# Attention and squared-ReLU MLP on one core: pinned weight splits, down-projection halves taken in turn two blocks apart, paced output sums

## The chip, the cores and the metric

The kernel runs as one program on 1 core of one Trainium2 chip. The metric is the time of one execution on the device, in microseconds (us). Of the kernel before there are three timed runs, from 2081.25 to 2085.26 us, with a median of 2083.21 us, and one profiled execution.

The engines are named as in the profile: PE (matmul), PEld (its weight loads), DVE (VectorE), ACT (ScalarE), POOL (GpSimd) and SP (SyncE, which here issues the loads).

## The reference

One layer: attention over an 8 x 64 grid of tokens, then an MLP with a squared ReLU. The change is in the MLP alone.

```python
D_MODEL, SEQ, MLP_HIDDEN = 2048, 512, 8192

def sq_relu_mlp(h, w1, w2):
    a = jax.nn.relu(h @ w1)
    return (a * a) @ w2

x = x + neighbourhood_attention(rms_norm(x, norm_mix), ...)
x = x + sq_relu_mlp(rms_norm(x, norm_mlp), mlp_w1, mlp_w2)
```

## The kernel before

**Number format.** All matmuls work on float32 values that are split in two parts, h (a rounded copy) and l (the rest), and each product is three matmuls: h·h, h·l and l·h. So every weight tile has to be split on the chip before PE can use it: ACT writes `wh` (line 233), DVE writes `wl` (line 235).

**The MLP in pairs.** Both projections are cut in a form of Strassen's scheme with seven products instead of eight (M1 to M7). A *pair* (class `Pair`) makes two column tiles of the result, 2 x 512 columns, for all 512 tokens. Its inner dimension is cut into *blocks* of four row tiles; for each block and each of the seven products there is one *chunk*, which is 12 matmuls (line 248). A pair goes through two stages: first M1, M5, M6, M4 for each of its blocks, and then M2, M3, M7 for each. With four blocks that is 28 chunks. The products share PSUM banks x, z, y and w (table `BANK`); at the last block of a product its bank is evicted (`evict`). M5, M6, M4 and M7 take a sum of weight quarters that is kept up as a chain (table `CHAIN`): DVE adds the quarter just loaded and the sum of the product before it in place, in line 217, before the split. So 4 of the 7 chunks of a block need this *add* (16 of the 28 in a pair).

**Up projection.** Pairs h0 to h7 multiply by `w1`, each with four blocks. Their results go through the ReLU, are turned on PE by eight small tasks per pair (`left_window`, run by `window()` in the second stage of the next pair), squared, and written by POOL to `z_t` in DRAM as sixteen blocks, two per pair, together with the sums that Strassen's left side needs.

**Down projection.** The sixteen blocks of z are used four at a time: `zc[c]` for c = 0 to 3. For each c there are two pairs, one for each half of the output's columns, named in the trace as tiles of `y`: y0_0, y0_1, y1_0, ... y3_1. After each chunk of y0_1, y1_1 and y2_1 (and of h7, for c = 0), `pass_on` loads the z tile that will take the place of the one just used for the last time: SP loads `zr` (line 759, 128 x 512), and six steps later `split_left` splits it as ACT's `a_z...h` (line 554) and DVE's `a_z...l` (line 556). So h7, y0_1, y1_1 and y2_1 carry 28 such loads and splits each, the other pairs none. Here such a pair is called a pair *with hand-over*.

**Output.** Every pair of c = 0 to 2 adds its eight output tiles to `y_sum` in DRAM with an accumulating DMA from POOL (line 748), as soon as each is evicted. The pairs of c = 3 read `y_sum` back (`prefetch`), add it and write `out`.

**What sets the order.** The program is written as chunks with side tasks that are due some *steps* later; a chunk is four steps. `run` issues the weight loads six chunks ahead and starts a split three chunks ahead. In `split_raw` the add is written first, `wh` five steps later and `wl` two steps after that. But the order in which instructions stand on each engine is not the written one: a scheduler sorts them, except those marked by `kept`, which keep the program's order. Before, `kept` has an effect only in the first 32 steps of the program.

**Buffers.** Weights land in the pool `raw` (10 tiles of 128 x 1024), split weights are in `hl` (3 pairs), and almost all else, the z tiles and the output tiles included, is in `tiles` (70 tiles of 128 x 512).

```python
def split_raw(u, i, first):
    ...
        if m in u.CHAIN:
            nc.vector.tensor_tensor(out=s, in0=s, in1=u.raw[u.CHAIN[m], b], op=ALU.add)
        yield 5 * STEP
    h = hl.tile([P, 2, T], F32R, tag="wh", name=f"wh_{name}")
    l = hl.tile([P, 2, T], F32R, tag="wl", name=f"wl_{name}")
    ...
        kept(nc.scalar.activation(h, s, AF.Copy))
        yield 2 * STEP
        kept(nc.vector.tensor_tensor(out=l, in0=s, in1=h.bitcast(F32), op=ALU.subtract))
```

Of the kernel before, what the change touches and what calls it, by code (L numbers as in the profile page):

```python
# [25 lines left out]
NCH = HID // D  # L26
# [6 lines left out]
NB = KT // 4  # L33
# [8 lines left out]
STEP, WAIT, PAIR = 1, 5, 3  # L42


class Unit:
# [7 lines left out]
    def __init__(self, name, src, act, done, kind):  # L53
        self.name, self.src, self.act, self.done, self.kind = name, src, act, done, kind
        self.n = KT // 4 if kind == "narrow" else KT
        self.raw, self.parts, self.ps = {}, {}, None
        self.load, self.before, self.after, self.lag = None, None, None, 0


class Pair:  # L60
# [19 lines left out]
    def __init__(self, name, w, row, col, comb, take):  # L80
        self.name, self.w, self.row, self.col, self.comb, self.take = name, w, row, col, comb, take
        self.raw, self.parts, self.banks, self.after = {}, {}, {}, None
        self.t, self.u, self.p4, self.p5 = {}, {}, {}, {}

    def chunks(self):
        return [(self, (m, b)) for stage in (self.FIRST, self.SECOND) for b in range(NB) for m in stage]

    def quarter(self, m, b):
        r, c = self.QUARTER[m]
        r, c = self.row + (4 * b + 2 * r) * P, self.col + c * T  # L90
        return self.w[r // (2 * P), c // T]


# [1 line left out]
def natten_mlp_kernel(ctx, tc, x_t, gains, w_qk, w_v, bias, w_o, w1, w2, out_t):  # L95
    nc = tc.nc
# [8 lines left out]
    def wtile(name, dt=F32):  # L105
        return tiles.tile([P, T], dt, tag="w", name=name)
# [6 lines left out]


    pinned = 4 * 8
    pos = [0]
# [92 lines left out]
    def split_raw(u, i, first):  # L209
        if not isinstance(u, Pair) and i % 2:  # L210
            return
        name = f"{u.name}_{i[0] if isinstance(u, Pair) else i}"
        s = u.raw[i]
        if isinstance(u, Pair):
            m, b = i
            if m in u.CHAIN:
                nc.vector.tensor_tensor(out=s, in0=s, in1=u.raw[u.CHAIN[m], b], op=ALU.add)  # L217
            yield 5 * STEP
        h = hl.tile([P, 2, T], F32R, tag="wh", name=f"wh_{name}")
        l = hl.tile([P, 2, T], F32R, tag="wl", name=f"wl_{name}")  # L220
        if isinstance(u, Pair):
            u.parts[i] = (h, l)
        else:
            u.parts[i], u.parts[i + 1] = (h[:, 0], l[:, 0]), (h[:, 1], l[:, 1])
        if first:
            kept(nc.vector.tensor_copy(out=h[:, 0], in_=s[:, 0]))
            kept(nc.vector.tensor_tensor(out=l[:, 0], in0=s[:, 0], in1=h[:, 0].bitcast(F32), op=ALU.subtract))
            enter_x(0)
            kept(nc.scalar.activation(h[:, 1], s[:, 1], AF.Copy))
            kept(nc.vector.tensor_tensor(out=l[:, 1], in0=s[:, 1], in1=h[:, 1].bitcast(F32), op=ALU.subtract))  # L230
            enter_x(1)
        else:
            kept(nc.scalar.activation(h, s, AF.Copy))  # L233
            yield 2 * STEP
            kept(nc.vector.tensor_tensor(out=l, in0=s, in1=h.bitcast(F32), op=ALU.subtract))  # L235

    def multiply_pair(u, i):
        m, b = i
        x = u.BANK[m]
        if x not in u.banks:  # L240
            u.banks[x] = [bank(f"{x}_{u.name}_{j}") for j in range(2)]
        wh, wl = u.parts.pop(i)
        ah, al = u.comb[b][m]
        for k in range(2):
            for j in range(2):
                c = slice(k * HALF + j * P, k * HALF + (j + 1) * P)
                for n, (a, w) in enumerate(((ah, wh), (ah, wl), (al, wh))):
                    nc.tensor.matmul(out=u.banks[x][j], lhsT=a[:, c], rhs=w[:, k],  # L248
                                     start=(m in u.FIRST and b + k + n == 0), stop=(b == NB - 1 and k == 1 and n == 2),
                                     skip_group_check=True)  # L250
                pos[0] += 1
                if 2 * k + j < 3:
                    run_side(pos[0])
        if b == NB - 1:
            start(evict(u, m))
        if u.after is not None:
            u.after(m, b)
        run_side(pos[0])
# [153 lines left out]
    class Head:  # L412
        def __init__(self, h):
            self.h = h
            self.p = {}
# [105 lines left out]
    for g in range(NG):  # L521
        u = Unit(f"v{g}", lambda i, g=g: w_v[i // 2, g], xa, v_done(g), "tokens")
# [36 lines left out]

# [44 lines left out]
    def window():  # L604
        if windows:
            windows.pop(0)()
# [118 lines left out]
    def take_out(p, last):  # L725
        ys = {}

        def prefetch():
            for c in range(QB):
                for half in range(2):  # L730
                    ys[c, half] = wtile(f"ys_{p}_{c}_{half}")
                    nc.sync.dma_start(out=ys[c, half], in_=y_sum[c, 2 * p + half])

        def take(c, half, src, add, minus=False):
            rows, cols = slice(c * P, (c + 1) * P), slice((2 * p + half) * T, (2 * p + half + 1) * T)
            if add is not None:
# [12 lines left out]
        return take, prefetch  # L749

    def pass_on(dst, block):


        order = (2, 4, 1, 5, 6, 3, 7)
        loaded = {}

        def load(m, b):
            t = loaded[m, b] = wtile(f"zr{m}_z{block}_{b}")
            nc.sync.dma_start(out=t.rearrange("p (k n) -> p k n", k=2), in_=z_t[4 * block + b][:, order.index(m)])

        def split_left(m, b):
            yield from parts_of(dst[b], m, loaded.pop((m, b)).rearrange("p (k n) -> p k n", k=2), f"a{m}_z{block}_{b}")
# [6 lines left out]
    pairs, comb = [], xc  # L769
    for p in range(FP):  # L770
        u = Pair(f"h{p}", w1, 0, 2 * p * T, comb, take_hidden(p))
        pairs.append(u)
    zc = [[{} for _ in range(NB)] for _ in range(NCH)]
    for c in range(NCH):
        for p in range(2):
            take, prefetch = take_out(p, c == NCH - 1)
            u = Pair(f"y{c}_{p}", w2, c * D, 2 * p * T, zc[c], take)
            u.prefetch = prefetch if c == NCH - 1 else None
            pairs.append(u)
    for n, u in enumerate(pairs):  # L780
        hand = None
        if n >= FP - 1 and (n - FP + 1) % 2 == 0 and n < len(pairs) - 1:
            block = (n - FP + 1) // 2
            hand = pass_on(zc[block], block)

        def after(m, b, n=n, u=u, hand=hand):
            if m in u.SECOND:
                if n == 0 and m == 2 and b == 0:
                    start(norm_a())
                window()  # L790
            if m == 4 and b == NB - 1 and n >= FP and u.prefetch is not None:
# [59 lines left out]
```

## Time and profile before

| | |
|---|---|
| Median of 3 runs | 2083.21 us (2081.25 to 2085.26) |
| Profiled execution, its time | 2081.29 us |
| Its span | 2079.5 us |
| PE busy | 2044.1 us, 98% of the span, 9330 matmuls |
| DVE busy | 1546.5 us, 74% |
| ACT busy | 1045.5 us, 50% |
| POOL busy | 116.7 us, 6% |
| Mean granted TensorE clock | 0.995 of full speed |
| Read and written in HBM | 348.14 MB and 50.33 MB |

The profiled execution lies 1.9 us below the median. Its time is 1.8 us more than its span, which runs from the first to the last instruction of the program. A matmul's busy time is modelled and overlaps the next one, so PE's busy share does not tell how fast it goes; the time from the first matmul of a pair to the first of the next one does.

### The profile page before, as it was taken

To read this page: it belongs to the slowest core of one execution; us is meant where nothing else is said; L and a number is where in the kernel's file an instruction comes from. 1 tells how busy PE (TensorE), PEld (TensorE's weight loads), DVE (VectorE), ACT (ScalarE), POOL (GpSimd) and SP (SyncE) were. 2 spreads that over 40 slices of the span, in tenths; PEclk is the share of its full clock that TensorE was granted. 3 is DMA by queue.
4 is the path that set the end of the run, shared out by engine and by line. 5 is a ranking of instruction groups with operands and counts; after the bars stand their busy time and mean duration, and the time that the engine had idled before them with its cause. 6 is when DMAs were issued, how large, how long until landed. Compare 5 with 4: busy or idle time off the path is not lost. (4 is left out here: it accounts for less than half of the span.)

```text
span 2079.5 us, 25226 instructions
## 1 busy us (share of the span) xinstructions
PE 2044.1 (98%) x9330; PEld 1684.3 (81%) x9330; DVE 1546.5 (74%) x1884; ACT 1045.5 (50%) x1412; POOL 116.7 (6%) x166
## 2 busy tenths in 40 slices
PE   9999999999999999999999999999989999999998
PEld 7888888888888888888888888887877877778787
DVE  6674674774774469778878878798879778779786
ACT  6663563653663445544545545565445445346333
POOL 0000000000000000010110110100201011010000
PEclk9999999999999999999999999999999999999999
DMA  7222222222233346565866757778689598688874
GB/s 289 101 92 83 100 92 92 96 90 96 99 101 127 112 137 211 193 217 199 274 202 226 269 180 255 270 255 304 226 295 286 187 272 279 204 261 278 256 243 147
DMA packets 127900, 400.15 MB, mean 192 GB/s; under 512 B 15008, under 2 KB 15008, under 8 KB 127776
## 3 DMA queue, kind: packets, MB, share of 16 engines
q1 hardware_dynamic: 110736, 352.37, 50.3%
q0 software_dynamic: 16896, 46.15, 7.8%
q8 instruction: 73, 1.20, 0.2%
q14 instruction: 51, 0.42, 0.1%
q10 hardware_dynamic: 144, 0.02, 0.0%
HBM read 348.14 MB, written 50.33 MB: 192 GB/s over the span
## 5 line engine op out<-in xcount | busy, mean ns | idle before, releaser
L233 ACT ACTIVATE wh_h<-w_h 128x1024 fp32r<-128x1024 f32 x224 | 237.6, 1060 | 275.0 <-PE y_h L248 83.7
L233 ACT ACTIVATE wh_y<-w_y 128x1024 fp32r<-128x1024 f32 x224 | 236.5, 1059 | 234.2 <-PE y_y L248 69.0
L235 DVE TENSOR_TENSOR wl_h<-w_h,wh_h 128x1024 fp32r<-128x1024 f32 x224 | 272.8, 1221 | 77.4 <-ACT wh_h L233 76.7
L235 DVE TENSOR_TENSOR wl_y<-w_y,wh_y 128x1024 fp32r<-128x1024 f32 x224 | 271.0, 1219 | 24.5 <-ACT wh_y L233 24.0
L217 DVE TENSOR_TENSOR w_y<-w_y,w_y 128x1024 f32<-128x1024 f32 x128 | 156.1, 1220 | 70.9 <-DMA w_y<-in_w 68.1
L217 DVE TENSOR_TENSOR w_h<-w_h,w_h 128x1024 f32<-128x1024 f32 x128 | 155.1, 1219 | 42.9 <-DMA w_h<-in_w 42.8
L235 DVE TENSOR_TENSOR wl_o<-w_o,wh_o 128x1024 fp32r<-128x1024 f32 x32 | 39.1, 1223 | 58.7 <-ACT wh_o L233 58.6
L233 ACT ACTIVATE wh_o<-w_o 128x1024 fp32r<-128x1024 f32 x32 | 33.9, 1059 | 80.0 <-PE mm_o L302 66.2
L233 ACT ACTIVATE wh_q<-w_q 128x1024 fp32r<-128x1024 f32 x32 | 34.0, 1062 | 77.8 <-PE mm_q L302 30.2
L235 DVE TENSOR_TENSOR wl_q<-w_q,wh_q 128x1024 fp32r<-128x1024 f32 x32 | 39.2, 1225 | 43.6 <-ACT wh_q L233 42.3
L235 DVE TENSOR_TENSOR wl_k<-w_k,wh_k 128x1024 fp32r<-128x1024 f32 x32 | 39.1, 1222 | 37.9 <-ACT wh_k L233 37.9
L233 ACT ACTIVATE wh_k<-w_k 128x1024 fp32r<-128x1024 f32 x32 | 34.0, 1062 | 50.8 <-PE mm_q L302 31.1
L233 ACT ACTIVATE wh_v<-w_v 128x1024 fp32r<-128x1024 f32 x31 | 32.8, 1058 | 47.4 <-PE mm_v L302 23.4
L235 DVE TENSOR_TENSOR wl_v<-w_v,wh_v 128x1024 fp32r<-128x1024 f32 x31 | 37.9, 1223 | 23.0 <-ACT wh_v L233 22.6
L600 POOL DMA_DIRECT2D y<-x1t_0s x4 | 2.3, 583 | 770.1 <-ACT x1t_0s L599 770.1
L711 POOL DMA_DIRECT2D z<-zt x32 | 17.7, 553 | 453.0 <-ACT zt L706 452.9
L554 ACT ACTIVATE a_z_0h<-zr_z 128x512 fp32r<-128x512 f32 x28 | 17.6, 627 | 50.4 <-DMA zr_z<-z 48.5
L509 ACT ACTIVATE t<-t,st 128x256 f32<-128x256 f32 x64 | 32.0, 501 | 10.6 <-DVE st L505 10.6
L706 ACT ACTIVATE zt<-zt 128x512 f32<-128x512 f32 x64 | 37.1, 580 | 0.0
L248 PE MATMUL y_y<-wl_y,a_z_1h 128*128 128x512 f32 x64 | 26.6, 416 | 8.4 <-DVE wl_y L235 8.4
L248 PE MATMUL z_y<-wl_y,a_z_0h 128*128 128x512 f32 x64 | 26.7, 418 | 6.8 <-DVE wl_y L235 6.8
L554 ACT ACTIVATE a_z_3h<-zr_z 128x512 fp32r<-128x512 f32 x28 | 17.5, 626 | 29.6 <-DMA zr_z<-z 29.6
(1435 smaller groups left out, 6304.2 us busy)
## 6 DMA issues: line engine op xcount, KB each, us to landing
w_h<-in_w SPq DMA_DIRECT2D x224, 512.0 KB, 4.3
w_y<-in_w SPq DMA_DIRECT2D x224, 512.0 KB, 4.6
zr_z<-z SPq DMA_DIRECT2D x112, 256.0 KB, 5.3
w_q<-in_w_qk SPq DMA_DIRECT2D x32, 512.0 KB, 3.5
w_k<-in_w_qk SPq DMA_DIRECT2D x32, 512.0 KB, 3.5
w_o<-in_w_o SPq DMA_DIRECT2D x32, 512.0 KB, 3.5
w_v<-in_w_v SPq DMA_DIRECT2D x31, 512.0 KB, 3.5
z<-zt POOLq DMA_DIRECT2D x32, 256.0 KB, 3.9
```

The source lines that it names most:

```text
L217: nc.vector.tensor_tensor(out=s, in0=s, in1=u.raw[u.CHAIN[m], b], op=ALU.add)
L233: kept(nc.scalar.activation(h, s, AF.Copy))
L235: kept(nc.vector.tensor_tensor(out=l, in0=s, in1=h.bitcast(F32), op=ALU.subtract))
L248: nc.tensor.matmul(out=u.banks[x][j], lhsT=a[:, c], rhs=w[:, k], start=(m in u.FIRST and b + k + n == 0), stop=(b == NB - 1 and k == 1 and ...
L509: nc.scalar.activation(halves[i], halves[i], AF.Exp, bias=st[:, i:i + 1], accum_out=st[:, 2 + i:3 + i])
L554: nc.scalar.activation(view(h), src, AF.Copy)
L600: nc.gpsimd.dma_start(out=dst, in_=t)
L706: nc.scalar.activation(t[:, i], ps, AF.Square)
L711: nc.gpsimd.dma_start(out=dst[:, 2], in_=t[:, 0, :HALF])
```

## The change

Three things are changed, all in the MLP.

1. **Order.** From the first weight split of a pair on, the adds, `wh`, `wl` and the two splits of z are marked `kept`, so that on their engines they stand in the order in which the program writes them. The step from the add to `wh` is 4 instead of 5.
2. **Blocks.** The down projection has nine pairs instead of eight, and the halves of the columns take turns two blocks apart: y0 takes blocks 0 and 1, y1 takes 0 to 3 (the other half), y2 takes 2 to 5, y3 4 to 7, and so on to y7 with 12 to 15 and y8 with 14 and 15. So y0 and y8 have 14 chunks and the rest 28; the sum is 224 as before. Of the blocks of y1 to y6 the first two are used there for the last time, and only their chunks (14 of 28) load and split a z tile for four blocks later. In h7, blocks 2 and 3 are loaded 48 steps later than before. The split comes 14 steps after the load instead of 6.
3. **Outputs.** The accumulating DMAs are put in a list, and `send` issues one after each chunk, with a wait on the newest matmul. Seven pairs do this now instead of six: 56 DMAs instead of 48.

```diff
     def kept(ins):
-        return tc.keep_in_program_order(ins) if pos[0] < pinned else ins
+        return tc.keep_in_program_order(ins) if pos[0] < pinned or in_pairs else ins
...
             m, b = i
+            in_pairs[:] = [True]
             if m in u.CHAIN:
-                nc.vector.tensor_tensor(out=s, in0=s, in1=u.raw[u.CHAIN[m], b], op=ALU.add)
-            yield 5 * STEP
+                kept(nc.vector.tensor_tensor(out=s, in0=s, in1=u.raw[u.CHAIN[m], b], op=ALU.add))
+            yield 4 * STEP
...
-        nc.scalar.activation(view(h), src, AF.Copy)
+        kept(nc.scalar.activation(view(h), src, AF.Copy))
         yield STEP
-        nc.vector.tensor_tensor(out=view(l), in0=src, in1=view(h).bitcast(F32), op=ALU.subtract)
+        kept(nc.vector.tensor_tensor(out=view(l), in0=src, in1=view(h).bitcast(F32), op=ALU.subtract))
...
             else:
-                nc.gpsimd.dma_start(out=y_sum[c, 2 * p + half], in_=t, accum_op=ALU.add)
+                outs.append((y_sum[c, 2 * p + half], t))
...
+    def send():
+        if outs:
+            dst, t = outs.pop(0)
+            ins = nc.gpsimd.dma_start(out=dst, in_=t, accum_op=ALU.add)
+            tc.add_manual_dep(ins.ins, newest[0].ins.name,
+                              mybir.DependencyInfo(mybir.DependencyClass.Sync, mybir.DependencyReason.DATA),
+                              reason="pace")
...
         def after(m, b):
-            load(m, b)
-            later(6 * STEP, lambda: start(split_left(m, b)))
+            if b in heirs:
+                wait = 48 * STEP if heirs[b] == b >= 2 else 0
+                later(wait, lambda: load(m, heirs[b]))
+                later(wait + 14 * STEP, lambda: start(split_left(m, heirs[b])))
...
+    for n in range(2 * NCH + 1):
+        p, c = 1 - n % 2, 2 * n - 2
+        rows = range(max(c, 0), min(c + NB, NCH * NB))
+        take, prefetch = take_out(p, n >= 2 * NCH - 1)
+        u = Pair(f"y{n}", w2, rows, 2 * p * T, zc, take)
...
+        c = 2 * (n - FP) - 2
+        if n == FP - 1:
+            hand = pass_on({b: b for b in u.blocks})
+        elif n > FP and c + NB < NCH * NB:
+            hand = pass_on({c: c + NB, c + 1: c + NB + 1})
...
+            send()
```

How the order moves is shown at two places. A row is an instruction's line, its operation and its tiles; `w_y1_0_5` is the weight tile of M5 in pair y1_0, `wl_y1_0_5` its l part, and the last number grows with the order in which the program was written. Line numbers after the change are those of the changed file: 217 has become 219, 233 and 235 are 235 and 237, 554 and 556 are 559 and 561, and 759 is 775.

The first place is DVE in the first stage of a pair in the down projection. Before, in pair y1_0, where the rows are the `wl` of block 1 (line 235) and adds (line 217) of the blocks 2 and 3:

```order
L235 TENSOR_TENSOR wl_y1_0_1_13272<-w_y1_0_1_13149,wh_y1_0_1_13271 128x1024
L217 TENSOR_TENSOR w_y1_0_5_13284<-w_y1_0_5_13284,w_y1_0_1_13263 128x1024
L235 TENSOR_TENSOR wl_y1_0_5_13293<-w_y1_0_5_13179,wh_y1_0_5_13292 128x1024
L217 TENSOR_TENSOR w_y1_0_6_13305<-w_y1_0_6_13305,w_y1_0_5_13284 128x1024
L217 TENSOR_TENSOR w_y1_0_5_13361<-w_y1_0_5_13361,w_y1_0_1_13342 128x1024
L235 TENSOR_TENSOR wl_y1_0_6_13312<-w_y1_0_6_13210,wh_y1_0_6_13311 128x1024
L217 TENSOR_TENSOR w_y1_0_4_13324<-w_y1_0_4_13324,w_y1_0_6_13305 128x1024
L235 TENSOR_TENSOR wl_y1_0_4_13330<-w_y1_0_4_13239,wh_y1_0_4_13329 128x1024
```

Here the `wl` of M6 of block 1 stands behind the add of M5 of block 3, which is seven chunks later in the program. The same stage after the change, in pair y2:

```order
L219 TENSOR_TENSOR w_y2_6_12971<-w_y2_6_12971,w_y2_5_12947 128x1024
L237 TENSOR_TENSOR wl_y2_5_13042<-w_y2_5_12947,wh_y2_5_13041 128x1024
L561 TENSOR_TENSOR a4_z_6l_13056<-zr4_z_6_12969,a4_z_6h_13055 128x512
L219 TENSOR_TENSOR w_y2_4_12997<-w_y2_4_12997,w_y2_6_12971 128x1024
L237 TENSOR_TENSOR wl_y2_6_13067<-w_y2_6_12971,wh_y2_6_13066 128x1024
```

Now each add stands just ahead of the `wl` of the chunk before it.

The second place is the z tiles of the hand-over, on SP, where they are loaded, and on ACT, where they are split. Before, in pair y0_1, SP has them between the weights:

```order
L193 DMA w_y0_1_6_12593<-in_w2 128x1024
L193 DMA w_y0_1_4_12618<-in_w2 128x1024
L759 DMA zr6_z1_0_12564<-z_4_129 128x512
L193 DMA w_y0_1_1_12642<-in_w2 128x1024
L759 DMA zr4_z1_0_12591<-z_4_129 128x512
```

And ACT, in the same pair, has their splits between the `wh`:

```order
L233 ACTIVATE wh_y0_1_1_12547<-w_y0_1_1_12441 128x1024
L554 ACTIVATE a5_z1_0h_12580<-zr5_z1_0_12537 128x512
L233 ACTIVATE wh_y0_1_5_12574<-w_y0_1_5_12465 128x1024
L554 ACTIVATE a6_z1_0h_12605<-zr6_z1_0_12564 128x512
L233 ACTIVATE wh_y0_1_6_12599<-w_y0_1_6_12490 128x1024
```

The tile `zr6_z1_0` is loaded after the weights of M4 of block 2 and split on ACT after the `wh` of M5 of block 1: SP is six chunks further on in the program than ACT. After the change, in pair y2, SP has them four in a row:

```order
L194 DMA w_y2_1_12923<-in_w2 128x1024
L194 DMA w_y2_5_12947<-in_w2 128x1024
L775 DMA zr1_z_6_12898<-z_6_131 128x512
L775 DMA zr5_z_6_12921<-z_6_131 128x512
L775 DMA zr6_z_6_12945<-z_6_131 128x512
L775 DMA zr4_z_6_12969<-z_6_131 128x512
L194 DMA w_y2_6_12971<-in_w2 128x1024
```

And ACT in pair y2:

```order
L235 ACTIVATE wh_y2_4_12992<-w_y2_4_12900 128x1024
L559 ACTIVATE a5_z_6h_13005<-zr5_z_6_12921 128x512
L235 ACTIVATE wh_y2_1_13016<-w_y2_1_12923 128x1024
L559 ACTIVATE a6_z_6h_13030<-zr6_z_6_12945 128x512
L235 ACTIVATE wh_y2_5_13041<-w_y2_5_12947 128x1024
L559 ACTIVATE a4_z_6h_13055<-zr4_z_6_12969 128x512
```

The tile `zr6_z_6` is loaded after the weights of a chunk of M5, and ACT has that chunk's `wh` right behind the split of `zr6_z_6`: the distance is one chunk.

## Rows read from the trace of the kernel before

**Rows 1.** Timeline of PE, start and length in us: first and last matmul of the down projection.
```profile
1419.65 0.39 PE L248 MATMUL x_y<-wh_y,a_z_0h 128*128 128x512 f32 x1
...
2073.29 0.39 PE L248 MATMUL y_y<-wh_y,a_z_3l 128*128 128x512 f32 x1
```
**Rows 2.** Windows, one per pair, h6 to y3_1: length, busy us, granted clock, DMA share, GB/s.
```profile
1258.54:1338.59 80.05, 80.05 (x369) 66.18 (x368) 63.58 (x72) 39.63 (x46) 8.15 (x12) 1.00 0.69 230
1338.59:1419.65 81.06, 81.06 (x370) 65.61 (x368) 76.23 (x94) 51.32 (x69) 8.15 (x12) 1.00 0.84 296
1419.65:1502.18 82.53, 81.06 (x369) 65.87 (x368) 69.27 (x80) 40.81 (x49) 11.27 (x16) 1.00 0.71 245
1502.18:1587.89 85.71, 78.89 (x338) 64.44 (x336) 74.54 (x84) 45.86 (x58) 5.64 (x7) 0.96 0.92 295
1587.89:1667.71 79.82, 77.36 (x337) 62.62 (x336) 60.61 (x60) 33.18 (x34) 7.75 (x10) 1.00 0.71 212
1667.71:1753.54 85.83, 80.23 (x337) 64.44 (x336) 72.29 (x80) 45.78 (x58) 6.22 (x8) 0.96 0.89 278
1753.54:1834.07 80.53, 77.66 (x338) 62.77 (x336) 61.36 (x61) 32.82 (x35) 8.02 (x10) 1.00 0.72 214
1834.07:1918.59 84.52, 79.59 (x338) 63.75 (x337) 72.16 (x80) 45.88 (x58) 5.95 (x7) 0.98 0.91 281
1918.59:1997.16 78.57, 77.03 (x338) 62.85 (x336) 66.59 (x70) 31.94 (x33) 5.24 (x6) 1.00 0.80 251
1997.16:2073.67 76.51, 76.51 (x337) 62.74 (x335) 55.94 (x59) 28.70 (x28) 0.00 (x0) 1.00 0.54 188
```
**Rows 3.** Waits of PE from 1419.65 us on: us in total, times, longest.
```profile
PE y_y L248 <- DVE wl_y L235: 10.4, 10, 2.1
PE z_y L248 <- DVE wl_y L235: 6.8, 2, 4.2
PE y_y L248 <- ACT wh_y L233: 5.6, 1, 5.6
```
**Rows 4.** Waits of DVE and ACT from 1419.65 us on.
```profile
DVE w_y L217 <- DMA w_y<-in_w: 67.9, 37, 5.4
...
ACT a_z_0h L554 <- DMA zr_z<-z: 44.1, 14, 11.0
...
ACT a_z_3h L554 <- DMA zr_z<-z: 29.6, 16, 4.9
```
**Rows 5.** Timelines of ACT, PE and DVE: two stalls, with the idle time before.
```profile
1522.60 0.63 ACT L554 ACTIVATE a_z_0h<-zr_z 128x512 fp32r<-128x512 f32 x1 [10.99 <-DMA zr_z<-z]
...
1524.23 0.80 PE L248 MATMUL y_y<-wh_y,a_z_1h 128*128 128x512 f32 x1 [5.57 <-ACT wh_y L233]
...
1604.63 1.22 DVE L217 TENSOR_TENSOR w_y<-w_y,w_y 128x1024 f32<-128x1024 f32 x1 [4.00 <-DMA w_y<-in_w]
...
1607.04 0.50 PE L248 MATMUL y_y<-wl_y,a_z_1h 128*128 128x512 f32 x1 [2.07 <-DVE wl_y L235]
```
**Rows 6.** DMA issues: KB each, median us from issue to landing; then z's extremes.
```profile
w_y<-in_w SPq DMA_DIRECT2D x224, 512.0 KB, 4.6
...
y<-p_y POOLq DMA_DIRECT2D x12, 256.0 KB, 11.2
...
DMA to landing us min/median/max: 2.6/5.3/17.9
```
**Rows 7.** Waits of the queue on SP over the whole span.
```profile
SPq L193 <- DVE wl_y L235: 423.7, 186, 8.1
```
**Rows 8.** Groups on DVE from 1419.65 us on: busy us, mean ns of one.
```profile
L235 DVE TENSOR_TENSOR wl_y<-w_y,wh_y 128x1024 fp32r<-128x1024 f32 x224 | 271.0, 1219 | 24.5 <-ACT wh_y L233 24.0
...
L556 DVE TENSOR_TENSOR a_z_3l<-zr_z,a_z_3h 128x512 fp32r<-128x512 f32 x24 | 16.4, 683 | 3.0 <-ACT a_z_3h L554 2.9
...
L672 DVE TENSOR_TENSOR t_y<-y_y,t_y 128x512 f32<-128x512 f32 x16 | 10.9, 683 | 1.3 <-PE y_y L248 1.3
```
**Rows 9.** Window with the highest traffic, columns as in rows 2.
```profile
1500.00:1550.00 50.00, 43.17 (x180) 34.89 (x179) 40.28 (x44) 23.04 (x29) 5.23 (x6) 0.93 0.96 306
```

More of the change, by code (lines that the diff above doesn't have):

```diff
@@ L78, with __init__ @@
     CHAIN = {5: 1, 6: 5, 4: 6, 7: 3}
-    def __init__(self, name, w, row, col, comb, take):
-        self.name, self.w, self.row, self.col, self.comb, self.take = name, w, row, col, comb, take
+    def __init__(self, name, w, blocks, col, comb, take):
+        self.name, self.w, self.blocks, self.col, self.comb, self.take = name, w, blocks, col, comb, take
         self.raw, self.parts, self.banks, self.after = {}, {}, {}, None
@@ L85, in chunks @@
     def chunks(self):
-        return [(self, (m, b)) for stage in (self.FIRST, self.SECOND) for b in range(NB) for m in stage]
+        return [(self, (m, b)) for stage in (self.FIRST, self.SECOND) for b in self.blocks for m in stage]
     def quarter(self, m, b):
         r, c = self.QUARTER[m]
-        r, c = self.row + (4 * b + 2 * r) * P, self.col + c * T
+        r, c = (4 * b + 2 * r) * P, self.col + c * T
         return self.w[r // (2 * P), c // T]
@@ L235, in split_raw @@
             kept(nc.vector.tensor_tensor(out=l, in0=s, in1=h.bitcast(F32), op=ALU.subtract))
+    newest = [None]
     def multiply_pair(u, i):
@@ L247, in multiply_pair @@
                 for n, (a, w) in enumerate(((ah, wh), (ah, wl), (al, wh))):
-                    nc.tensor.matmul(out=u.banks[x][j], lhsT=a[:, c], rhs=w[:, k],
-                                     start=(m in u.FIRST and b + k + n == 0), stop=(b == NB - 1 and k == 1 and n == 2),
-                                     skip_group_check=True)
+                    newest[0] = nc.tensor.matmul(out=u.banks[x][j], lhsT=a[:, c], rhs=w[:, k],
+                                                 start=(m in u.FIRST and b == u.blocks[0] and k + n == 0),
+                                                 stop=(b == u.blocks[-1] and k == 1 and n == 2),
+                                                 skip_group_check=True)
                 pos[0] += 1
@@ L253, in multiply_pair @@
                     run_side(pos[0])
[L254 removed]
+        if b == u.blocks[-1]:
             start(evict(u, m))
@@ L747, in take, with pass_on @@
             else:
-                nc.gpsimd.dma_start(out=y_sum[c, 2 * p + half], in_=t, accum_op=ALU.add)
+                outs.append((y_sum[c, 2 * p + half], t))
         return take, prefetch
-    def pass_on(dst, block):
+    outs = []
+    def send():
[5 more added lines that the diff above has]
+                              reason="pace")
+    def pass_on(heirs):
         order = (2, 4, 1, 5, 6, 3, 7)
@@ L757, in load @@
         def load(m, b):
-            t = loaded[m, b] = wtile(f"zr{m}_z{block}_{b}")
-            nc.sync.dma_start(out=t.rearrange("p (k n) -> p k n", k=2), in_=z_t[4 * block + b][:, order.index(m)])
+            t = loaded[m, b] = wtile(f"zr{m}_z_{b}")
+            nc.sync.dma_start(out=t.rearrange("p (k n) -> p k n", k=2), in_=z_t[b][:, order.index(m)])
         def split_left(m, b):
-            yield from parts_of(dst[b], m, loaded.pop((m, b)).rearrange("p (k n) -> p k n", k=2), f"a{m}_z{block}_{b}")
+            yield from parts_of(zc[b], m, loaded.pop((m, b)).rearrange("p (k n) -> p k n", k=2), f"a{m}_z_{b}")
@@ L764, in after @@
         def after(m, b):
-            load(m, b)
-            later(6 * STEP, lambda: start(split_left(m, b)))
-        return after
-    pairs, comb = [], xc
-    for p in range(FP):
-        u = Pair(f"h{p}", w1, 0, 2 * p * T, comb, take_hidden(p))
-        pairs.append(u)
[L773 to L779, printed above, removed]
@@ L780, in natten_mlp_kernel @@
-    for n, u in enumerate(pairs):
[L781 to L784, printed above, removed]
+            if b in heirs:
+                wait = 48 * STEP if heirs[b] == b >= 2 else 0
+                later(wait, lambda: load(m, heirs[b]))
+                later(wait + 14 * STEP, lambda: start(split_left(m, heirs[b])))
+        return after
+    pairs = [Pair(f"h{p}", w1, range(NB), 2 * p * T, xc, take_hidden(p)) for p in range(FP)]
@@ new lines, in natten_mlp_kernel @@
+    zc = [{} for _ in range(NCH * NB)]
+    for n in range(2 * NCH + 1):
[3 more added lines that the diff above has]
+        u = Pair(f"y{n}", w2, rows, 2 * p * T, zc, take)
+        u.prefetch = prefetch if n >= 2 * NCH - 1 else None
+        pairs.append(u)
+    for n, u in enumerate(pairs):
+        c = 2 * (n - FP) - 2
[3 more added lines that the diff above has]
+            hand = pass_on({c: c + NB, c + 1: c + NB + 1})
+        else:
+            hand = None
@@ L790, in after @@
                 window()
-            if m == 4 and b == NB - 1 and n >= FP and u.prefetch is not None:
+                if n == FP and m == 7:
+                    window()
+            if m == 4 and b == u.blocks[-1] and n >= FP and u.prefetch is not None:
                 u.prefetch()
```

1 line of the change is left out of this document (added).

## The prediction

> **What bounds the kernel now.** I read the profile in four steps. First the windows by pair, since PE's busy share of 98% hides how fast it goes. From the first matmul of the down projection to the last [rows 1] there are eight pairs of 28 chunks. The last of them, y3_1, takes 76.51 us at full clock, PE idle nowhere: 2.733 us per chunk. An up-projection pair such as h6 takes 80.05 us, which is the same plus eight tasks that turn tiles, and y0_0 carries such tasks too (h7's). Against these two, the pairs lose [rows 2]: h7 1.0 us, y0_0 2.5, y0_1 9.2, y1_0 3.3, y1_1 9.3, y2_0 4.0, y2_1 8.0, y3_0 2.1; together 39.4 us. The pairs with hand-over lose most, and show DVE busy for 72 to 75 us and 278 to 295 GB/s; in three of them the granted clock is below 1.
>
> Second, PE's waits: 25.3 us in five groups, the largest three of which are shown [rows 3]; all are for `wl` or `wh`. Half clock (1.2 GHz instead of 2.4) adds 8.5 us: a mean of 0.96 over 85.7 us costs 3.4 us, twice, and 0.98 over 84.5 us costs 1.7 us [rows 2]. The remaining 5.6 us are steps too short to be listed as waits.
>
> Third, why `wl` and `wh` were late: neither DVE nor ACT was too slow, they stood still. DVE waited 67.9 us for weights in adds, ACT 44.1 us and 29.6 us for z tiles in the two largest groups of splits [rows 4]. Fourth, two stalls in order of time [rows 5]: ACT stands for 10.99 us before a z split, the `wh` behind it is late, and PE idles 5.57 us. DVE stands for 4.00 us before an add, the `wl` behind it is late, and PE idles 2.07 us. So the bound is the place of two kinds of instruction on engines that work in order: each waits for a transfer in front of work that PE needs sooner. The rest of the kernel is PE at its pace.
>
> **The change, part by part.** *The adds.* A weight load can start when the `raw` tile ten chunks earlier is free, that is after its `wl`; SP waits mostly for that [rows 7]. Counted over the whole order of the down projection, 75 of the 128 adds stood eight or nine chunks ahead of the last `wl` before them, which leaves 10 - 9 to 10 - 8 chunks, 2.7 to 5.5 us, between issue and add. The median landing takes 4.6 us [rows 6], hence the waits. Now all 128, and the up projection's 127 that have a `wl` before them, stand exactly two ahead: eight chunks, 21.9 us.
>
> *The z tiles.* They are issued behind a weight load on SP, so the same count holds. Before, 64 of 112 had SP seven chunks further than ACT at the split, leaving three chunks or 8.2 us, against a median landing of 5.3 us and a longest of 17.9 us [rows 6]. Now the largest distance is five (36 of 112): 13.7 us, and 76 have four or fewer, 16.4 us and more.
>
> *Blocks two apart.* Hand-over work moves from three pairs of the down projection to six, 14 splits in each. DVE's busy time in a pair with hand-over is 74.5 us, in the pair after it 60.6 us [rows 2]; half of each makes 67.6 us in a 76.5 us pair. A chunk with hand-over in the first stage costs DVE 1.22 for `wl`, 0.75 x 1.22 for adds (an add takes what a `wl` takes: same shape and operation) and 0.68 for the split [rows 8], 2.82 us against 2.73 us. Eight such chunks in a row put DVE 0.7 us behind, then it catches up; before there were sixteen. I take 0, with 0.7 us x 6 = 4 us as the upper end.
>
> *Outputs.* One more pair means 12 more evictions on DVE of 0.68 us [rows 8], 8.2 us over the whole phase, beside the 9 us that DVE is idle in every pair: 0 on the path. It also means eight more accumulating DMAs. The pace moves the eight of a pair from its end into the first eight chunks of the next one. POOL waits at each send. Behind it wait other sends, and near the end of y0 the writes of z block 15, which is loaded in y6 at the earliest. An output tile stays up to 21.9 us longer, plus 11.2 us to land [rows 6]; z loads of the next pair's second block reuse such tiles, so SP may wait here with weight loads behind it. Lower end 0, as the loads have 13.7 us and more to spare; upper end under the last rival.
>
> *Where PE's own order moves.* In h0, y0, y1 and y8 the scheduler now interleaves two chunks, and `wh` is due up to a chunk earlier. None of it is in the trace; the nearest row is a pair without hand-over, which loses 2.1 to 4.0 us [rows 2]. Four places, so 0 to 16 us; I take 2 us in all, nearer the lower end, because each of the four places is only a few chunks long, and a whole pair loses 2.1 to 4.0 us. Nothing can be gained.
>
> *The rest.* The up projection gains at most h7's 1.0 us; h6 and its like already run without a stall and DVE has 16 us idle in each, so pins there cost 0, or a few us if an add meets a late load. y8 has six chunks, 16.4 us, left after the loads of `y_sum` instead of twelve; y3_1 lost nothing with twelve. From the last matmul to the span's end (6.2 us) nothing changes.
>
> *Sum.* The profiled execution took 2081.3 us. 2081.3 - 39.4 + 2.0 = 2043.9 us. The median of the runs lies 1.9 us higher; some of that spread comes from stalls that go, so I say **2045 us**.
>
> *A row weighed against the skill.* In the window with the highest traffic the DMA engines were busy for 0.96 and moved 306 GB/s [rows 9], and accumulates took 11.2 us where weights took 4.6 us [rows 6]. So accumulates, issued by POOL, and loads, issued by SP, share one limit here. In the first eight chunks of y1 to y6 a chunk now has a weight load, a z load and an accumulate, 0.524 + 0.262 + 0.262 = 1.05 MB in 2.733 us: 384 GB/s. The Trainium skill, DMA: Bandwidth & Descriptors, section "Issuing engines are not separate DMA queues", says that DMAs run on the same 16 engines and interleave whichever engine starts them. The trace agrees, with 0.96 busy in that window; by that rule the pace does not take the outputs out of the way of the z loads, which is the first rival. Without it the sum stays at 2045 us.
>
> **The rivals.**
>
> 1. *A DMA backlog in the first eight chunks.* Above 306 GB/s there is 78 GB/s too much for 21.9 us: 1.7 MB, 5.6 us late. If an accumulate's reading of its target counts as well, the load is 480 GB/s and the backlog 12.4 us. z would land 5.3 + 5.6 = 10.9 to 17.7 us after issue, against 13.7 us at the shortest. So nothing is lost at the lower end, and up to 4 us per pair at the upper, again with half clock behind it. For it: y0_1, where landings of 17.9 us and the worst stall fall together. Against: before, that pair went on with z loads for 28 chunks; now 8 follow with weights alone. I price it as the loss of a pair without hand-over now, 3.0 us on average over the four, for six pairs: 18 us, so 2063 us. With 4 us and a half clock of 3.4 us in five or six of them, some 2085 us is the end.
> 2. *The pins do not bring the order to bear*, because evictions and turned tiles are unpinned and still stand in front. Then the losses stay: 2083 us. Against: the counts above are of the whole order, and evictions wait for PE, not for DMAs.
> 3. *Slower: outputs hold the tiles that z loads need.* Place: SP, in the second four z loads of y1 to y6 and the weights queued behind them. With 11.2 us landings there is room; it decides when an accumulate takes so long that the 21.9 us lead of the weights is used up, at around 30 us from send to landing. At twice the longest z landing, 36 us, PE would idle 6 us or more and then lose 3.4 us at half clock; with the weights behind also late, some 10 to 14 us per pair, 60 to 84 us over six: 2105 to 2129 us. Against: no accumulate in the trace has a median over 11.2 us, in bursts of eight; paced they come one per 2.7 us.
>
> **How the numbers follow.** Forecast (2040 to 2054 us): 0.78. Backlog (2054 to 2085, likeliest 2063): 0.15. Order without effect: 0.03. Slower: 0.04. The first two are faster by far more than 0.2% (4 us, about what a measurement of this kernel can tell from no change), so faster 0.93, same 0.03, slower 0.04. The lower end of the range is the fastest run less all of the 39.4 us, 2081.25 - 39.4 = 2041.9, and two more since 28 chunks may go at 76.2 us: 2040. The upper end takes in a third of the backlog case: 2062.
>
> **What would show it.** In the profile after: seven full pairs at 76.5 to 77.5 us each and y0 and y8 at half, DVE's wait for weights in adds down from 67.9 us to below 10, ACT's for z below 10, a granted clock of 1.00 in the whole phase, DVE at about 67 us in each full pair. The backlog would show as ACT waits for z in the first eight chunks of a pair, with landings over 13 us; the last rival as SP waits for accumulates. The prediction is wrong if the gap of the down projection stays over 15 us against 224 chunks at 2.733 us plus the tasks, or if an up-projection pair takes more than 80.3 us.

## The result and the profile after

The changed kernel takes **2046.72 us** (median of 4 runs, 2045.76 to 2047.55); the kernel before, timed beside it, 2082.38 us (2081.25 to 2085.26). The ratio is 0.983, with an interval of 0.981 to 0.984. The forecast was 2045 us.

The profiled execution of after took 2047.55 us with a span of 2045.7 us. Its windows by pair (columns as in [rows 2]: length, busy us of PE, PEld, DVE, ACT and POOL, granted clock, DMA share, GB/s) are h0, h1, h7, y0 (half a pair), y1, y2, y4, y7 and y8 (half a pair):

```profile
779.92:860.90 80.98, 79.85 (x358) 64.80 (x357) 68.36 (x74) 45.01 (x57) 2.16 (x4) 1.00 0.63 206
860.90:940.95 80.05, 80.05 (x369) 66.20 (x368) 65.09 (x73) 39.63 (x47) 8.18 (x12) 1.00 0.62 205
...
1341.22:1421.28 80.06, 80.06 (x370) 66.20 (x369) 72.64 (x88) 46.80 (x62) 8.16 (x12) 1.00 0.80 284
1421.28:1465.02 43.74, 42.43 (x202) 34.37 (x200) 42.44 (x53) 29.22 (x41) 7.53 (x11) 1.00 0.74 265
1465.02:1544.38 79.36, 77.66 (x340) 62.77 (x339) 70.39 (x82) 40.57 (x50) 9.44 (x12) 1.00 0.93 312
1544.38:1620.56 76.18, 76.18 (x337) 63.06 (x336) 66.62 (x71) 39.19 (x46) 6.77 (x8) 1.00 0.86 270
1696.75:1772.93 76.18, 76.18 (x338) 63.08 (x336) 66.62 (x71) 39.19 (x46) 6.79 (x8) 1.00 0.84 267
1925.29:2001.48 76.19, 76.19 (x337) 63.06 (x336) 62.96 (x64) 30.84 (x30) 5.09 (x6) 1.00 0.80 248
2001.48:2039.56 38.08, 38.08 (x169) 31.34 (x167) 34.70 (x41) 13.84 (x14) 0.00 (x0) 1.00 0.51 180
```

From y2 on PE stands nowhere and every pair takes 76.18 us, with hand-over or without; before, the pairs with hand-over took 84.5 to 85.8 us [rows 2]. The granted clock is 1.00 in every window. The waits of PE from 1400 us on, which answer to [rows 3], are four short groups of 2.9 us in all, against 25.3 us:

```profile
PE y_y L252 <- DVE wl_y L237: 1.2, 2, 1.0
PE z_y L252 <- DVE wl_y L237: 1.0, 1, 1.0
PE w_y L252 <- DVE wl_y L237: 0.4, 1, 0.4
PE y_y L252 <- ACT wh_y L235: 0.3, 1, 0.3
```

Among DVE's waits over the same stretch, the one for weights in adds, 67.9 us before [rows 4], is the second row. What DVE now waits for is the `wh` in front of a `wl`, two engines in step with no transfer between them:

```profile
DVE wl_y L237 <- ACT wh_y L235: 68.2, 81, 1.5
DVE w_y L219 <- DMA w_y<-in_w: 1.7, 1, 1.7
```

Among ACT's waits no group of z splits waits for z any more; before, the two largest were 44.1 and 29.6 us. The loads did not become faster at the median. The DMA issues (KB, median us to landing), and z's minimum, median and maximum, answer to [rows 6]:

```profile
w_y<-in_w SPq DMA_DIRECT2D x224, 512.0 KB, 5.1
zr_z<-z SPq DMA_DIRECT2D x112, 256.0 KB, 5.6
...
y<-p_y POOLq DMA_DIRECT2D x14, 256.0 KB, 7.6
...
DMA to landing us min/median/max: 3.7/5.6/13.8
```

Weights and z land a little later than before (5.1 and 5.6 us against 4.6 and 5.3), and PE hardly notices, because they are asked for earlier in relation to their use. What did become shorter is the longest landing of a z tile (13.8 us against 17.9) and the median of the paced accumulates (7.6 us against 11.2 in this group).

**Where the time came from.** The span fell from 2079.5 to 2045.7 us, 33.8 us. The down projection gave 35.7 of them: it took 2073.67 - 1419.65 = 654.0 us before and 2039.56 - 1421.28 = 618.3 us now. h7 gave 1.0 us (81.06 to 80.05). Three things took back 2.9 us: h0 to h6 together take 0.8 us more, the first matmul of h0 comes 1.8 us later (timeline, 779.92 against 778.09 us; e4 and e10 below, whose code up to there is that of the changed kernel, have 778.31 and 778.28, so this is not the change), and the stretch behind the last matmul is 0.3 us longer.

### The profile page after: what moved, and what is told of

It reads as the page before. It is cut to its first block, busy times and chain, and to the rows that moved or that the text cites. A ratio compares the mean times of both kernels' runs of the same rounds, so it can differ in the third digit from the quotient of the medians.

```text
span 2045.7 us, 25293 instructions
## 1 busy us (share of the span) xinstructions
PE 2033.4 (99%) x9330; PEld 1683.9 (82%) x9330; DVE 1555.5 (76%) x1896; ACT 1046.8 (51%) x1416; POOL 122.7 (6%) x174
## 4 chain that ended last, share of the span: by engine, by line
PE 96%; DMA 2%; DVE 1%; issue 1%; POOL 0%; ACT 0%; SPq 0%; DVEq 0%; POOLq 0%; ACTq 0%
PE mm_v L307 9%; PE mm_q L307 9%; PE mm_k L307 9%; PE mm_o L307 8%; PE y_h L252 8%; PE x_h L252 8%; PE z_h L252 8%; PE y_y L252 8%; PE z_y L252 8%; PE x_y L252 8%; PE w_h L252 4%; PE w_y L252 4%; PE zt L705 1%; PE o L474 1%; PE pt L459 1%; DMA w_y<-in_w 1%
## 5 line engine op out<-in xcount | busy, mean ns | idle before, releaser
L716 POOL DMA_DIRECT2D z<-zt x32 | 18.1, 565 | 440.1 <-ACT zt L711 440.1
L762 POOL DMA_DIRECT2D y<-c x14 | 12.3, 882 | 353.1 <-PE x_y L252 340.2
L715 POOL DMA_DIRECT2D z<-zt x32 | 22.7, 710 | 75.4 <-ACT zt L711 75.4
L252 PE MATMUL y_h<-wl_h,a_x1h 128*128 128x512 f32 x64 | 25.0, 391 | 0.9 <-DVE wl_h L237 0.9
L252 PE MATMUL y_h<-wh_h,a_x1h 128*128 128x512 f32 x64 | 25.6, 403 | 0.2 <-ACT wh_h L235 0.2
```

The source lines that it names most:

```text
L252: newest[0] = nc.tensor.matmul(out=u.banks[x][j], lhsT=a[:, c], rhs=w[:, k], start=(m in u.FIRST and b == u.blocks[0] and k + n == 0), sto ...
L715: nc.gpsimd.dma_start(out=dst[:, 0:2], in_=t[:, 1].rearrange("p (m n) -> p m n", m=2))
L716: nc.gpsimd.dma_start(out=dst[:, 2], in_=t[:, 0, :HALF])
```

## The experiments

Theory: only two leads count, that of the adds over the `wl` in front of them (set by the pins) and that of the z load over its split (6 or 14 steps, and the pins). Rivals: the halves must take turns, the outputs must be paced, or one of the two leads follows from the other. "Before" was timed beside each; its medians were 2081.4 to 2082.0 us.

| run | pairs | pins | z steps | us | ratio, interval |
|---|---|---|---|---|---|
| e1_pins | old | all | 6 | 2057.37 | 0.988 (0.987 to 0.990) |
| e2_lead14 | old | none | 14 | 2067.96 | 0.993 (0.992 to 0.995) |
| e6_pins14 | old | all | 14 | 2044.96 | 0.982 (0.981 to 0.984) |
| g1_pinadds14 | old | weights | 14 | 2046.44 | 0.982 (0.980 to 0.984) |
| g2_pinz14 | old | z | 14 | 2072.00 | 0.994 (0.992 to 0.997) |
| g3_pins18 | old | all | 18 | 2043.80 | 0.981 (0.979 to 0.983) |
| e3_nopins | new | none | 14 | 2078.60 | 0.998 (0.997 to 1.000) |
| e5_lead6 | new | all | 6 | 2063.23 | 0.991 (0.990 to 0.993) |
| e10_lead10 | new | all | 10 | 2048.31 | 0.984 (0.982 to 0.986) |
| e4_nopace | new, unpaced | all | 14 | 2046.69 | 0.983 (0.982 to 0.985) |
| f1_pepin | new | all, and PE | 14 | 2049.53 | 0.984 (0.983 to 0.986) |

### One part alone, in the kernel before

**e1_pins.** The pins and the four steps between add and `wh`, nothing else.

```diff
+        return tc.keep_in_program_order(ins) if pos[0] < pinned or in_pairs else ins
...
+                kept(nc.vector.tensor_tensor(out=s, in0=s, in1=u.raw[u.CHAIN[m], b], op=ALU.add))
+            yield 4 * STEP
...
+        kept(nc.scalar.activation(view(h), src, AF.Copy))
...
+        kept(nc.vector.tensor_tensor(out=view(l), in0=src, in1=view(h).bitcast(F32), op=ALU.subtract))
```

> The kernel before with the pins alone (adds, wh, wl and the z splits in the program's order, 4 steps from add to wh); pairs, 6-step lead of z and outputs as before. In its order all adds stand two chunks ahead, but 83 of the 112 z splits still have SP seven chunks further than ACT. Theory (leads decide): DVE's wait for weights in adds falls from 67.9 us to under 10, ACT's waits for z stay (70 to 110 us), and about half of the 39 us loss goes: 2055 to 2068 us. Rival (the even load of the new pairs is what counts, since DVE is busy 72 to 75 us of 76.5 in a pair with hand-over): 2072 us or more, with pairs with hand-over still at 83 us and more.

It gains 24.3 us. DVE's wait for weights in adds is gone from its list, but z stays late, though less than expected: ACT's wait for z, summed over its groups from 1400 us on, is 47.6 us, against 98.7 before and 70 to 110 expected. Most z splits stand where they stood, so why the pins alone halve it is open. A wait of ACT and one of PE in this kernel read

```profile
ACT a_z_0h L556 <- DMA zr_z<-z: 25.5, 8, 11.6
...
PE w_y L250 <- ACT wh_y L235: 6.2, 1, 6.2
```

One z split stood 11.6 us, and the `wh` behind it let PE stand 6.2 us: the first stall of [rows 5] without the second.

**e2_lead14.** The other half alone.

```diff
-            later(6 * STEP, lambda: start(split_left(m, b)))
+            later(14 * STEP, lambda: start(split_left(m, b)))
```

> The kernel before with one edit: the z split is begun 14 steps behind its load instead of 6. No pins, old pairs, outputs in bursts. Theory (two separate waits, z on ACT and weights on DVE): ACT's wait for z falls below 20 us, but 70 of 128 adds still stand eight or nine chunks ahead, so DVE's wait for weights stays at 50 us or more and the time at 2060 to 2078 us. Rival (the z splits were the root, and DVE's waits for weights followed from them): 2050 to 2057 us with DVE's wait for weights below 25 us.

It gains 13.4 us. The waits of DVE and ACT show the opposite of e1:

```profile
DVE w_y L217 <- DMA w_y<-in_w: 71.9, 48, 3.8
...
ACT a_z_0h L554 <- DMA zr_z<-z: 17.4, 5, 5.5
```

ACT's wait for z, summed over its groups, falls from 98.7 to 21.8 us (a little over the 20 expected), DVE's for weights does not fall. So DVE's wait does not follow from ACT's. The reverse does not hold in full: in e1 the pins without the lead took half of ACT's wait.

**e6_pins14.** Both, with the old pairs and the outputs in bursts: the diffs of e1 and e2 together.

> The kernel before with the pins, the add four steps ahead of its split and the z split 14 steps behind its load; the pairs and the outputs stay as they were (three pairs with hand-over, outputs in bursts of eight). Theory (only the leads of the adds and of the z splits in the engines' orders count; the blocks two apart are not needed for themselves): all adds stand two chunks ahead of the last wl, z splits five ahead for most, as in the changed kernel, so 2046 to 2052 us, ACT's wait for z below 10 us, the pairs with hand-over at 76.2 to 78 us. Rival (three pairs with hand-over are too much for DVE and the DMA engines, and the halves must take turns): 2055 us or more, with the second pairs of a block at 79 us and over.

It takes 2044.96 us, 36.4 us less than before and 1.0 us below the range expected; the two parts alone gave 24.3 + 13.4 = 37.7. This is the run that decides: with both leads, the kernel needs neither the new pairs nor the paced outputs. The windows of y0_1 and y1_1, two of the pairs with 28 hand-overs:

```profile
1501.82:1579.49 77.67, 77.38 (x337) 62.60 (x336) 70.93 (x79) 44.25 (x56) 6.65 (x8) 1.00 0.98 333
...
1656.14:1732.30 76.16, 76.16 (x337) 63.08 (x336) 70.97 (x79) 44.38 (x56) 6.69 (x8) 1.00 0.94 310
```

DVE does 71 us of work in y1_1, more than in any pair of after from y2 on, and PE does not stand. The rival of an even load falls.

**g1_pinadds14 and g2_pinz14.** Which pin? Both have 14 steps. g1 pins adds, `wh` and `wl` as e1 does, but not the two z splits; g2 pins the z splits alone and keeps five steps from add to `wh`. The cuts show g1 against e6 and g2 against the kernel before.

```diff
 g1:
-        kept(nc.scalar.activation(view(h), src, AF.Copy))
+        nc.scalar.activation(view(h), src, AF.Copy)
 ...
 g2:
-        nc.scalar.activation(view(h), src, AF.Copy)
+        (tc.keep_in_program_order if in_pairs else (lambda q: q))(nc.scalar.activation(view(h), src, AF.Copy))
 ...
-            later(6 * STEP, lambda: start(split_left(m, b)))
+            later(14 * STEP, lambda: start(split_left(m, b)))
```

> The kernel before with 14 steps between z load and z split, and only the weights' instructions (adds, wh, wl) pinned; the z splits are left to the scheduler. 113 of 128 adds of the down projection stand two chunks ahead, 15 three; z splits five or six for most, eight for two. Theory (each of the two leads counts by itself, and a pin on z splits is worth something only where it shortens their lead): as with all pins, 2044 to 2050 us, DVE's wait for weights below 5 us. Rival (z splits left free drift in front of wh again and stall ACT): 2052 us or more with ACT's wait for z above 15 us.

> The kernel before with 14 steps between z load and z split, and only the z splits pinned; adds, wh and wl are left to the scheduler, 70 of 128 adds eight or nine chunks ahead. Theory (the adds' lead makes DVE wait whatever the z splits do): DVE's wait for weights at 50 us or more and the time at 2060 to 2076 us, level with the lead of 14 steps alone (2068.0 us). Rival (pinned z splits are what frees the engines): 2046 to 2056 us.

g1 takes 2046.44 us, level with all pins; DVE's wait for weights is 0.3 us. g2 takes 2072.00 us, no better than the lead alone. Timelines of DVE and of PE in g2 show why:

```profile
1506.02 1.22 DVE L219 TENSOR_TENSOR w_y<-w_y,w_y 128x1024 f32<-128x1024 f32 x1
1515.06 1.23 DVE L219 TENSOR_TENSOR w_y<-w_y,w_y 128x1024 f32<-128x1024 f32 x1 [7.82 <-DMA w_y<-in_w]
1516.20 1.22 DVE L237 TENSOR_TENSOR wl_y<-w_y,wh_y 128x1024 fp32r<-128x1024 f32 x1
...
1517.47 0.80 PE L250 MATMUL x_y<-wl_y,a_z_1h 128*128 128x512 f32 x1 [5.55 <-DVE wl_y L237]
```

An add stands 7.82 us for its weight, the `wl` behind it ends at 1517.4 us, and PE, 5.55 us idle, starts at once. The Trainium skill, PSUM — Partial Sum Buffer, section "Engine vs sequencer instructions", says that the queues of ScalarE, VectorE and GpSimdE are strict FIFO; these rows agree for VectorE. So the scheduler's order of the weights' instructions cost most of the loss. It is the adds that stand waiting, but adds, `wh` and `wl` were always pinned together, so that a pin on the adds alone would do is not shown.

**g3_pins18.** e6 with four more steps of lead.

```diff
-            later(14 * STEP, lambda: start(split_left(m, b)))
+            later(18 * STEP, lambda: start(split_left(m, b)))
```

> The kernel before with all the pins and 18 steps between z load and z split (14 gave 2045.0 us): most z splits four chunks ahead instead of five, so 16.4 us of slack for the landing instead of 13.7 us. Theory (the longest z landings, 16 to 18 us, now have room, but with 14 steps ACT already waited for none of note): the same, 2043 to 2047 us. Rival (tiles held longer delay the weight loads behind them on SP): 2049 us or more with DVE waiting for weights again.

2043.80 us (2043.28 to 2044.49), the lowest median of all. Its y0_1 is free of stalls, and PE waits in one group only from 1400 us on:

```profile
1501.78:1577.94 76.16, 76.16 (x337) 63.06 (x336) 70.35 (x78) 43.95 (x55) 6.66 (x8) 1.00 1.01 339
```

```profile
PE y_y L250 <- DVE wl_y L237: 1.2, 4, 0.7
```

Against the change its interval (0.979 to 0.983) overlaps (0.981 to 0.984), and the two were not timed side by side, so that it is faster is likely and not shown. It needs nothing but pins and a longer lead.

### One part undone, in the changed kernel

**e3_nopins.** `in_pairs` stays empty, so nothing in the pairs is pinned.

```diff
-            in_pairs[:] = [True]
```

> The changed kernel without its pins: halves two blocks apart, z split 14 steps after its load, paced outputs, but the scheduler's order. Its adds stand eight or nine chunks ahead in 90 of 128 cases, as before. Theory (leads decide): DVE waits for weights 50 us or more, and every pair loses 2 to 5 us: 2058 to 2075 us. Rival (the even load counts): 2046 to 2050 us, no pair over 78 us.

2078.60 us: nearly the whole gain is gone, 3.6 us more than the theory's upper end. The four steps from add to `wh` are still in this kernel, so they are not what gained. DVE waits again, more often than before (37 times then):

```profile
DVE w_y L218 <- DMA w_y<-in_w: 83.5, 53, 3.8
```

ACT waits for z again too, 49.0 us over its groups, where the changed kernel has none, although the split is written 14 steps behind its load in both. Without pins SP is six or more chunks further than ACT at 46 or more of the 112 splits (counted in the trace's order), so the written steps are not the lead on the engine.

**e5_lead6.** The z split 6 steps behind its load, with pins.

```diff
-                later(wait + 14 * STEP, lambda: start(split_left(m, heirs[b])))
+                later(wait + 6 * STEP, lambda: start(split_left(m, heirs[b])))
```

> The changed kernel with the z split 6 steps after its load instead of 14. In its order 60 of 112 z splits have SP seven chunks further than ACT, a lead of 8.2 us. Theory (leads decide): landings of 8 to 14 us come too late in some pairs, ACT waits 15 to 40 us for z, 2049 to 2058 us. Rival (with the load spread over six pairs z lands in time anyway): 2044 to 2048 us, ACT's wait for z under 5 us.

2063.23 us, over the theory's 2058, and ACT waits 50.0 us for z, over the 15 to 40 expected. PE's largest wait of PE and the z split that caused it:

```profile
PE w_y L252 <- ACT wh_y L235: 8.6, 1, 8.6
...
ACT a_z_4h L559 <- DMA zr_z<-z: 11.1, 3, 10.1
```

The misses in time of e3 and e5 point the same way. With the old pairs, the same settings (no pins and 14 steps; pins and 6 steps) took 2067.96 and 2057.37 us: the new pairs and their paced outputs made it 10.6 and 5.9 us worse. Where a lead is too short, each pair with hand-over loses, and there are six of them instead of three. In e3, y1 to y6 take 80.5 to 82.7 us each, while in e2 only y0_1, y1_1 and y2_1 are over 77 us after y0_0 (81.2, 84.7 and 84.2).

**e10_lead10.** The same line with 10 steps.

> The changed kernel with the z split 10 steps behind its load, between 14 (the change, 2046.7 us) and 6 (2063.2 us). The largest distance between SP and ACT at a z split is six chunks for 48 of 112 (five for 36 of 112 with 14 steps, seven for 60 with 6 steps). Theory (the loss comes when a landing outlasts the slack of 10 minus that distance, here 10.9 us, and the longest z landings are 12 to 14 us): a few late z tiles, 2047 to 2056 us, ACT's wait for z 2 to 12 us. Rival (the lead of z no longer counts once adds are pinned, and 6 steps lost for another reason): 2063 us as with 6 steps.

2048.31 us: 6, 10 and 14 steps give 2063, 2048 and 2047 us. ACT waits 19.7 us for z, more than the 2 to 12 expected, but PE hardly suffers; y1 alone is longer (81.7 us). Probably the loss begins where a landing outlasts the lead and the slack of the `wh` behind it together, and I had left out the second; no run varies that slack alone.

**e4_nopace.** Outputs sent as soon as they are evicted.

```diff
-                outs.append((y_sum[c, 2 * p + half], t))
+                nc.gpsimd.dma_start(out=y_sum[c, 2 * p + half], in_=t, accum_op=ALU.add)
```

> The changed kernel with each output's accumulating DMA issued as soon as it is evicted, without a wait on a matmul. Theory (leads decide, and they are 13.7 us or more): landings of accumulates go up to 10 to 16 us, no wait of PE follows, 2044 to 2049 us. Rival (the pace is needed, or the backlog bites): ACT waits for z at the start of each pair, 2052 us or more.

2046.69 us, the time of the change. The pace does spread the accumulates; without it the last of a pair's four groups lands in

```profile
y<-p_y POOLq DMA_DIRECT2D x14, 256.0 KB, 13.3
```

instead of 7.6 us. But z lands in 5.8 us (median) against 5.6. The Trainium skill, DMA: Bandwidth & Descriptors, section "Issuing engines are not separate DMA queues", says that DMAs run on the same 16 engines and interleave whichever engine starts them; this agrees, as far as 0.2 us can tell.

**f1_pepin.** The matmuls of the pairs are kept in the program's order as well, so no chunks are interleaved.

```diff
-                    newest[0] = nc.tensor.matmul(out=u.banks[x][j], lhsT=a[:, c], rhs=w[:, k],
+                    newest[0] = kept(nc.tensor.matmul(out=u.banks[x][j], lhsT=a[:, c], rhs=w[:, k],
...
-                                                 skip_group_check=True)
+                                                 skip_group_check=True))
```

> The changed kernel with the matmuls of the pairs pinned to the program's order too, so that no two chunks are interleaved in h0, y0, y1 and y8 (448 unbroken chunks of 12 matmuls). Theory (the changed kernel still loses some 6 us in h0, y0 and y1, part of it because interleaved chunks want wh and wl up to a chunk earlier): h0 at 80.05 to 80.9, y0 at 41.7 to 43 and y1 at 76.2 to 78 us, 0 to 5 us less than the changed kernel: 2042 to 2047 us. Rival (those losses come from the traffic of the first z loads and of tasks that turn tiles, not from PE's order): no change, 2046 to 2048 us, or some us slower where a chunk held in order is the late one.

2049.53 us, no gain; in its profiled execution (2047.03 us, the fastest of four) h0 takes 81.57, y0 43.92 and y1 79.34 us, where after has 80.98, 43.74 and 79.36. The theory falls: what after still loses there is not the interleaving. That it is traffic, as the rival has it, this run does not show.

## Why the prediction was right

- **Adds and z tiles.** Right, and shown: pins on the adds and the longer z lead each free one engine (DVE in e1, most of ACT in e2 and all of it in g2), and together they give all of the gain (e6). The 39.4 us of losses were the right sum to start from: the down projection gained 35.7 us and h7 its 1.0 us, against 38.4 and 1.0 less the 2 us held back.
- **Half clock.** Gone with the stalls, as the sum assumed. The kernels with weights pinned and 14 or 18 steps show a mean of 0.998 to 1.000 in all their runs, the kernel before 0.993 to 0.997.
- **Blocks two apart.** Taken at 0 and measured at that: e6 without them is 1.8 us lower, with overlapping intervals. The argument for it (DVE 67.6 us in each pair instead of 74.5) came true, 66.62 us, and was worth nothing, since DVE has room for 71 us in a pair.
- **Outputs.** 0 for the eight more accumulates and the pace. The pace measured 0 (e4); the accumulates were not tried alone, and are within the 1.8 us between e6 and the change.
- **PE's order in h0, y0, y1 and y8.** The one term that was mis-sized, and its cause was wrong. I took 2 us; against a clean pair y0 loses 2.0, y1 3.2 and h0 0.9 us, y8 nothing: 6.1 us. f1 shows that interleaving is not why.

  *y0.* It is the pins: without them, and nothing else changed, y0 takes 41.71 us (e3), with them 43.3 to 43.9 us in five kernels. DVE has no idle time there. The adds of the first chunks, which in e3 are done before y0 begins, now stand among the evictions of h7, and PE idles for the `wl` behind them (e3 has that `wl` 2.9 us after y0's first matmul, after 6.4 us):

```profile
1425.31 1.22 DVE L219 TENSOR_TENSOR w_y<-w_y,w_y 128x1024 f32<-128x1024 f32 x1
...
1427.64 1.22 DVE L237 TENSOR_TENSOR wl_y<-w_y,wh_y 128x1024 fp32r<-128x1024 f32 x1
...
1428.91 0.50 PE L252 MATMUL y_y<-wl_y,a_z_0h 128*128 128x512 f32 x1 [1.03 <-DVE wl_y L237]
```

  *h0.* The pins again. All nine kernels with pinned weights take 80.9 to 81.0 us (f1 81.6), and in each PE waits in the first 19 us for a `wl_h`, 0.9 us in after. In the four others that wait is missing, and PE waits 1.2 to 2.4 us for the norm's `an` instead; they take 80.2 to 83.0 us. So one sign of being wrong that I had named came true: an up-projection pair over 80.3 us. There I had priced pins at 0 unless an add met a late load; none did, but DVE was busy without a gap ahead of that `wl_h`.

  *y1.* It is the window with the most traffic (0.93, 312 GB/s). The longest of its stalls stands behind an add that waited for its weight. That weight was asked for at 1478.4 us and took 11.7 us to land, after SP's weight loads had stood up to 6.2 us for writes of z (DVE, PE, and SP from 1462 to 1486 us):

```profile
1490.18 1.23 DVE L219 TENSOR_TENSOR w_y<-w_y,w_y 128x1024 f32<-128x1024 f32 x1 [1.66 <-DMA w_y<-in_w]
...
1492.60 0.50 PE L252 MATMUL z_y<-wl_y,a_z_2h 128*128 128x512 f32 x1 [1.01 <-DVE wl_y L237]
...
SPq L194 <- DMA z<-zt: 10.6, 2, 6.2
```

  So in y1 it is a weight that was late; no z split waited for z in after. In the old pairs y0_1 loses 1.5 us with 14 steps and nothing with 18; whether 18 steps would help y1 was not tried in the new pairs.
- **Clean pairs.** I had 76.5 us from y3_1; they take 76.18. Over some eight pairs that gives 2.6 us back and hides more than half of the error above. The sum was for the profiled execution, 2043.9 against 2047.55 us: 4.1 - 2.6, and 2.1 us from a later start of h0 and a longer end, neither of them in the sum, make 3.6 us. The medians, 2045 and 2046.72, are closer by luck: I had put the median above the profiled execution, which after the change is the slowest of the four runs.
- **Rival 1, the backlog.** Its premise was wrong. In the first eight chunks of y2 the engines are full and move 311 GB/s, but the 384 GB/s that I worked out were not asked for. The window, and the DMA issues in it:

```profile
1544.38:1566.24 21.86, 21.86 (x98) 18.09 (x97) 20.94 (x23) 10.57 (x12) 5.07 (x6) 1.00 1.08 311
...
w_y<-in_w SPq DMA_DIRECT2D x8, 512.0 KB, 9.3
zr_z<-z SPq DMA_DIRECT2D x4, 256.0 KB, 10.1
y<-u_y POOLq DMA_DIRECT2D x2, 256.0 KB, 7.9
y<-t_y POOLq DMA_DIRECT2D x2, 256.0 KB, 7.4
y<-p_y POOLq DMA_DIRECT2D x2, 256.0 KB, 7.4
...
DMA to landing us min/median/max: 9.2/10.1/10.9
```

  I had counted eight z loads and eight accumulates, from the program. On SP four of the z loads, and on POOL two of the accumulates, go out before the pair begins. What is left is 8 x 0.524 + 10 x 0.262 = 6.8 MB in 21.86 us, 312 GB/s, which is what moved. The four z tiles do land late, after 9.2 to 10.9 us (in y2 to y6 never over 11.1); the lead of 13.7 us covers that, and PE is busy for all of the 21.86 us. In y1 a little of the rival came true: there z tiles landed after up to 13.8 us, and the late weight above cost PE 1.0 us.
- **Rivals 2 and 3.** The pins did bring the order to bear. From 1400 us on the longest wait of SP for a `wl` to free a weight tile is 4.8 us, and no wait for an accumulate appears among SP's largest.

## What to carry to other kernels

Before spreading work evenly, look at what stands in front of the late instruction on its own engine: here DVE and ACT had time enough and waited for transfers in front of work that was due sooner, and pins on the weights' adds and splits and eight more steps of lead gave all of the gain (g1). Count a lead in places of the buffer pool, from the order on the engine and not from the program, and compare it with the longest landing, not the median. Count traffic from the engines' order too: the backlog counted from the program was never asked for. A rearrangement that shares the load among more stages multiplies a loss per stage if that loss is not cured first.

## What was not expected of the hardware

- The DMA engines carried more than I had taken for their limit: 339 GB/s over 76 us with PE at full pace (g3's y0_1), where the busiest 50 us of before moved 306 GB/s at a share of 0.96 [rows 9].
- Accumulating transfers of 256 KB land in 7.6 us when sent one per chunk and in 13.3 us at the end of a burst of eight, and neither moves the time.
- The first matmul of h0 comes 778.28, 778.31 and 779.92 us after the start in e10, e4 and after, whose code up to there is the same, so some 2 us of any difference here are not the change.
